# First adaptive modulation of a diffusion trunk: six chunks of 512 columns, or twelve pieces of 128, 256 and 512

## Chip, cores and metric

One core of a Trainium2 chip. The time is the device time of one execution in microseconds (us), median over runs of the same program. Inputs lie in HBM; the layout of the weights is prepared on the host ahead of the run and is not timed.

## What is computed

A trunk of four layers works on 256 context tokens and 256 latent tokens of 1024 features: a gated mixer (SGU), an RWKV7 layer, a latent attention (MLA), and a second SGU. Every layer starts in the same way, here cut to what matters for the first:

```python
def ada_modulation(cond, w, b):
    m = jax.nn.silu(cond) @ w + b            # w: 1024 x 3072
    shift, scale, gate = jnp.split(m, 3, axis=-1)
    return shift[..., None, :], scale[..., None, :], gate[..., None, :]
...
h  = rms_norm(x) * (1 + scale) + shift        # latent, from c
hc = rms_norm(ctx) * (1 + c_scale) + c_shift  # context, from c_ctx
...
u, v, z = jnp.split(h @ w_in, 3, axis=-1)     # w_in: 1024 x 6144
```

All arithmetic is float32. For the first layer the modulation needs the whole 12 MB weight matrix `ada_w[0]`, and nothing of the mixer can run before some block of `h` (128 of the 1024 features, for all 512 tokens) is there; that block needs its own 128 columns of shift and of scale.

## The kernel before, in words

Features lie on the 128 partitions, in 8 blocks `k`; the 512 tokens (256 context, 256 latent) lie along the free dimension. The kernel is written in a tile framework: the program is traced in Python order, and a list scheduler places the instructions of each engine by that order as priority and by its own estimate of when operands are ready. An engine then runs its list strictly in order, so an instruction that waits holds up what stands behind it. Tiles of one tag share a fixed number of buffers.

**Start (L1358 to L1381).** The queue of SP issues all loads: the condition, eight blocks of `xT` (256 KB each), small constants, then modulation weights and mixer weights in the order of the calls. `sq_add` sums the squares of the blocks; `norm_rstd` (L281) sums them over partitions with a matmul by ones (`ssq`) and takes the reciprocal root (`rstd`).

**Modulation (`ada_load` L201, `ada_first` L210).** `ada_w[0]` is cut into six chunks of 512 columns: chunks 0 and 1 are the shift, 2 and 3 the scale, 4 and 5 the gate. A chunk (2 MB) comes in four transfers of 512 KB, each with two of the eight `k` blocks of all 512 columns. In `ada_first` each `k` block is a matmul with the condition as stationary operand (128 x 32), in column tiles of 32, four `k` at a time into four groups of 32 partitions (`adap`, L218). ScalarE copies the result to SBUF (`m4`, L221); four matmuls with `sel2` add the four groups and transpose 128 columns each into one shared PSUM tile (`adaT`, L225); VectorE adds the bias (L228), and 1.0 for the scale (L230). The profile counts each float32 matmul as two instructions: 16 for a chunk, 8 for its transposes.

**Normalized blocks (`norm_mod` L288).** For each `k`: VectorE multiplies `xT` by `rstd` (L292); ScalarE scales and shifts the context half (L297), VectorE the latent half (L295); `split` makes the two parts of a split-float pair `hp`: a rounded part on ScalarE (L304), the rest on VectorE (L305).

**Weights (`wload` L170, `wparts` L173).** Each 1 MB of mixer weights is loaded into `raw` (3 buffers in this phase), then split into `hi` (ScalarE, L183) and `lo` (VectorE, L184), each with 2 buffers.

**First mixer, projection `v` (`sgu` L349).** Four column blocks `c` of 512, each in two halves of four `k`. For each `k` and each of four token blocks there are three matmuls (L375 to L377, tile `pv`): 48 a half, 96 a column block, 384 in all. The calls order the modulation so: `first` (L1367) runs chunks 0 and 2 and then issues the loads of chunks 1 and 3; blocks 0 to 3 are made; the first half runs; `early` runs chunks 1 and 3 and blocks 4 to 7 are made (L366 to L368); the second half runs. `later` (L1371) does the gate's chunks 4 and 5 much later. `ada_rest` (L232) computes the other layers' modulation on VectorE beside the first mixer.

Of the kernel before, what the change touches and what calls it, by code (L numbers as in the profile page):

```python
# [8 lines left out]
F32 = mybir.dt.float32  # L9
# [6 lines left out]
D = 1024  # L16
KD = 8
T = 512
RMS_EPS = 1e-6


def fm_tiles(w, kb, ob):
# [14 lines left out]
def layout(inp):  # L37
    a = {k: np.asarray(v) for k, v in inp.items()}
    o = {}
    f = np.float32  # L40
    o["xT"] = np.concatenate([a["ctx"][0], a["x"][0]], 0).T.reshape(KD, 128, T).transpose(1, 0, 2)
    o["cond"] = np.stack([cols(a["c_ctx"]), cols(a["c"][0])], -1)
    o["ada_w0"] = a["ada_w"][0].reshape(KD, 128, 6, 512).transpose(2, 1, 0, 3).reshape(6, 128, KD * 512)
    o["ada_wT"] = a["ada_w"][1:4].transpose(0, 2, 1).reshape(3, 12, 2, 128, D).transpose(0, 1, 3, 2, 4).reshape(3, 12, 128, 2 * D)
    o["condr"] = np.stack([a["c_ctx"], a["c"][0]])[None]
    o["ada_b"] = np.stack([cols(a["ada_b"][i]) for i in range(4)], 1)
    for j in range(2):
        w = a["sgu_w_in"][j]
        o[f"sgu_u{j}"] = fm_tiles(w[:, 0:2048], 8, 2)
        o[f"sgu_v{j}"] = tm_tiles(w[:, 2048:4096], 4)  # L50
        o[f"sgu_z{j}"] = fm_tiles(w[:, 4096:6144], 8, 2)
        o[f"sgu_o{j}"] = np.concatenate([fm_tiles(a["sgu_w_out"][j][i * D:(i + 1) * D], 8, 2) for i in range(2)])
        o[f"sgu_gain{j}"] = cols(a["sgu_gain"][j])
        o[f"sgu_ws{j}"] = a["sgu_w_s"][j].transpose(2, 0, 1)
        o[f"sgu_bs{j}"] = np.broadcast_to(a["sgu_b_s"][j][None], (128, 8, 128))
    for c, nm in ((0, "r"), (1, "k"), (3, "z")):
        o["rw_" + nm] = fm_tiles(a["rwkv_w_in"][0, c], 8, 2)
    o["rw_v"] = tm_tiles(a["rwkv_w_in"][0, 2], 4)
    o["rw_o"] = fm_tiles(a["rwkv_w_out"][0], 8, 2)
    for nm in "wa":  # L60
        o[f"rw_{nm}1"] = fm_tiles(a[f"rwkv_{nm}_lora1"][0].transpose(1, 0, 2).reshape(D, 128), 8, 1)
        o[f"rw_{nm}2"] = np.tile(a[f"rwkv_{nm}_lora2"][0].transpose(1, 0, 2), (2, 1, 1))
    o["rw_vec"] = np.stack([cols(a["rwkv_mu"][0, c]) for c in range(6)]
                           + [cols(a["rwkv_w0"][0, n]) for n in range(2)] + [cols(a["rwkv_a0"][0, n]) for n in range(2)]
                           + [cols(a["rwkv_" + nm][0]) for nm in ("k_k", "k_a", "r_k", "ln_gain", "ln_bias")], 1)
    t64 = np.arange(64)
    strict, incl = (t64[:, None] < t64[None, :]).astype(f), (t64[:, None] <= t64[None, :]).astype(f)
    o["masks"] = np.tile(np.concatenate([strict, incl], 1), (2, 1))
    o["bd"] = np.kron(np.eye(2, dtype=f), np.ones((64, 64), f))
    w = a["mla_w_in"][0]  # L70
    o["ml_cq"] = fm_tiles(w[:, 0:768], 8, 1)
    o["ml_ckv"] = fm_tiles(w[:, 768:1024], 8, 1)
    wr = w[:, 1024:1088]
    o["ml_kr"] = fm_tiles(np.concatenate([wr, wr], 1), 8, 1)
    o["ml_z"] = fm_tiles(w[:, 1088:3136], 8, 1)
    uq = a["mla_w_uq"][0].reshape(768, 16, 192)
    o["ml_qn"] = fm_tiles(np.ascontiguousarray(uq[:, :, 0:128]).reshape(768, 2048), 6, 1)
    o["ml_qr"] = fm_tiles(np.ascontiguousarray(uq[:, :, 128:192]).reshape(768, 1024), 6, 1)
    ukv = a["mla_w_ukv"][0].reshape(256, 16, 256)
    o["ml_kv"] = np.concatenate([fm_tiles(np.ascontiguousarray(ukv[:, :, 0:128]).reshape(256, 2048), 2, 2),  # L80
                                 tm_tiles(np.ascontiguousarray(ukv[:, :, 128:256]).reshape(256, 2048), 2, 256)], 2)
    o["ml_o"] = np.concatenate([fm_tiles(a["mla_w_out"][0][i * D:(i + 1) * D], 8, 1) for i in range(2)])
    gq, gk = a["mla_qk_gain_q"][0], a["mla_qk_gain_k"][0]
    o["ml_vec"] = np.concatenate([cols(a["mla_q_norm"][0]), cols(a["mla_kv_norm"][0])]
                                 + [np.stack([g[0:128], np.tile(g[128:192], 2)], 1) for g in (gq, gk)], 1)
    ti = np.arange(256)
    inv = (10000.0 ** (-np.arange(16, dtype=f) / f(16))).astype(f)
    ang = np.concatenate([(ti // 64).astype(f)[:, None] * inv, (ti % 64).astype(f)[:, None] * inv], 1)
    o["rope"] = np.stack([np.tile(fn(ang).astype(f).T, (4, 1)) for fn in (np.cos, np.sin)], 1)
    sw = np.zeros((64, 64), f)  # L90
    sw[np.arange(32) + 32, np.arange(32)] = -1.0
    sw[np.arange(32), np.arange(32) + 32] = 1.0
    o["swap"] = np.kron(np.eye(2, dtype=f), sw)
    o["ident"] = np.eye(128, dtype=f)
    o["sel2"] = (np.arange(128)[:, None] % 32 == np.arange(2)[None, :]).astype(f)
    return {k: np.ascontiguousarray(v) for k, v in o.items()}


def body(tc, I, out):
    nc = tc.nc  # L100
# [4 lines left out]
    def ps(name, tag=None):  # L105
        tag = tag or env["ps"][0][0]
        return env["pp"].tile([128, 512], F32, tag=tag, name=name, bufs=dict(env["ps"])[tag])
# [93 lines left out]
    def ada_load(chunks):  # L201

        raws = {}
        for n in chunks:
            for q in range(4):
                raws[n, q] = env["a"].tile([128, 2, T], F32, tag="p", name="adaw", bufs=env["npair"])
                nc.sync.dma_start(out=raws[n, q].rearrange("p k c -> p (k c)"), in_=I["ada_w0"][n, :, q * 1024:q * 1024 + 1024])
        return raws

    def ada_first(chunks, raws):  # L210

        pt = ps("adaT")
        for n in chunks:
            pm = ps("adap")
            for h in range(2):
                for kk in range(4):
                    k = h * 4 + kk
                    PE.matmul(pm[32 * kk:32 * kk + 32, :], scp[:, k, :], raws[n, k // 2][:, k % 2, :],  # L218
                              start=(h == 0), stop=(h == 1), tile_position=(0, 32 * kk))
            m4 = at("m4")  # L220
            S.copy(m4, pm)  # L221
            yield
            for q in range(4):
                f = n * 4 + q
                PE.matmul(pt[:, 2 * f:2 * f + 2], m4[:, q * 128:(q + 1) * 128], sel2, start=True, stop=True)  # L225
            f = slice(n * 4, n * 4 + 4)
            for c in range(2):
                V.tensor_tensor(mods[0][:, f, c], pt[:, 0:48].rearrange("p (f c) -> p f c", c=2)[:, f, c], ada_b[:, 0, f], ALU.add)  # L228
            if n in (2, 3):
                V.tensor_scalar(mods[0][:, f, :], mods[0][:, f, :], 1.0, None, ALU.add)  # L230

    def ada_rest():  # L232
# [113 lines left out]
            yield  # L346


    def sgu(j, m, t0, done=None, first=None, early=None, later=(), head=None):  # L349
        later = iter(later)  # L350
        n = T - t0
        tbs = list(range(t0 // 128, 4))
        r = norm_rstd(t0)
        head = head or wload(I[f"sgu_v{j}"][0])
        if first:
            first()
        hs = [pair("hp") for _ in range(KD)]
        norm_mod(m, t0, hs, r, range(4 if early else 8))
        ss = const.tile([128, 4, 4], F32, tag="ss", name="ss")
        v = {}  # L360
        for c in range(4):
# [1 line left out]
                next(later, None)  # L363
            pv = {tb: ps("pv") for tb in tbs}
            for half in range(2):
                if early and (c, half) == (0, 1):  # L366
                    early()
                    norm_mod(m, t0, hs, r, range(4, 8))  # L368
                whi, wlo = wload(I[f"sgu_v{j}"][c * 2 + half]) if c + half else head
                for kk in range(4):  # L370
                    k = half * 4 + kk
                    for tb in tbs:
                        sl = slice(tb * 128, tb * 128 + 128)
                        ws_ = slice(kk * 512, kk * 512 + 512)
# [983 lines left out]
    with phase("0", 4, 20, 3):  # L1358
        scp = silu_cond()
        for k in range(KD):  # L1360
            sq_add(k, 0)
        act_set("natural_log_exp_and_others")
        raws = ada_load((0,))
        head0 = wload(I["sgu_v0"][0])
        raws.update(ada_load((2,)))

        def first():  # L1367
            interleave(ada_first((0, 2), raws))
            raws.update(ada_load((1, 3)))

        def later():  # L1371
            r4 = ada_load((4,))
            yield
            yield from ada_first((4,), r4)
            r5 = ada_load((5,))
            yield
            yield
            yield from ada_first((5,), r5)

        sgu(0, mods[0], 0, first=first, early=lambda: interleave(ada_first((1, 3), raws)), later=later(), head=head0)  # L1380
        for _ in ada_rest():  # L1381
            pass
    rwkv(mods[1])
# [21 lines left out]
```

## Time and profile before

| what | value |
|---|---|
| median of 3 runs | 1618.8 us (1617.66 to 1621.54) |
| profiled execution, its own time | 1616.74 us |
| its span (first to last instruction) | 1615.0 us |
| TensorE busy (PE) | 1516.5 us, 94% |
| VectorE busy (DVE) | 1151.3 us, 71% |
| ScalarE busy (ACT) | 788.0 us, 49% |
| mean granted clock of TensorE | 0.97 of full |

PE is TensorE, PEld its weight loads, DVE VectorE, ACT ScalarE, SP the engine that issues the transfers. L218 is line 218 of the kernel. Each row of a timeline gives the start and the duration in us, engine, line, operation, output<-input with the shape, the count, and in brackets how long the engine stood idle before and what ended that. Matmuls are pipelined, so their durations overlap; the distance of their starts is what they cost in a dense stream. PEclk is the granted clock as a share of 2.4 GHz; 0.50 is 1.2 GHz.

### The profile page before, as it was taken

How to read it: one execution, taken by the hardware profiler on the slowest of the kernel's cores; microseconds unless marked ns; L12 is line 12 of the kernel's file. 1: busy time of each engine (PE TensorE's matmuls, PEld its weight loads, DVE VectorE, ACT ScalarE, POOL GpSimd, SP SyncE). 2: the span in 40 equal slices, each digit the busy share in tenths (PEclk: the TensorE clock that was granted, in tenths of full speed). 3: DMA queues.
4: the chain of work that ended last, by engine and by line, in shares of the span. 5: the costliest groups of instructions: out<-in, count | busy, mean ns of one | idle time of the engine just before them, and what ended most of it. 6: DMA issues, size and time to landing. Idle time of an engine off the chain costs nothing.

```text
span 1615.0 us, 28890 instructions
## 1 busy us (share of the span) xinstructions
PE 1516.5 (94%) x11666; PEld 1173.8 (73%) x11666; DVE 1151.3 (71%) x2101; ACT 788.0 (49%) x1404; POOL 124.8 (8%) x156
## 2 busy tenths in 40 slices
PE   5999999999599998899899899899999999979998
PEld 2787888888467644777676677678777777768887
DVE  3789998845788367586796854778766666665876
ACT  4544231222455353444445333569866766456543
POOL 0000000000500142212303000000000000000000
PEclk8999999999799999799999999999999999989999
DMA  9676658631044553432433133134321232265452
GB/s 366 242 288 232 234 192 305 233 105 52 36 145 167 174 159 77 145 90 80 126 103 87 59 113 103 62 129 137 121 76 47 78 92 92 66 234 196 169 183 79
DMA packets 95174, 229.05 MB, mean 142 GB/s; under 512 B 26048, under 2 KB 52160, under 8 KB 80576
## 3 DMA queue, kind: packets, MB, share of 16 engines
q1 hardware_dynamic: 92736, 223.00, 41.1%
q10 hardware_dynamic: 2304, 4.20, 0.7%
q8 instruction: 92, 1.51, 0.4%
q14 instruction: 42, 0.34, 0.1%
HBM read 208.81 MB, written 17.83 MB: 140 GB/s over the span
## 4 chain that ended last, share of the span: by engine, by line
PE 46%; DVE 6%; ACT 6%; issue 1%; POOL 1%; DMA 0%; ACTq 0%; DVEq 0%; POOLq 0%
PE fm L310 4%; PE op L310 4%; PE pg L904 3%; PE op L975 2%; PE fm L311 2%; PE op L311 2%; PE pz L310 2%; PE pu L310 2%; PE po L1286 2%; PE sc L1304 2%; PE pe L790 2%; PE sc L1305 1%; PE pv L376 1%; PE pz L311 1%; PE pv L377 1%
## 5 line engine op out<-in xcount | busy, mean ns | idle before, releaser
L184 DVE TENSOR_TENSOR lo<-raw,hi 128x2048 fp32r<-128x2048 f32 (+3 forms) x147 | 247.2, 1683 | 105.0 <-ACT hi L183 104.4
L183 ACT CAST hi<-raw 128x2048 fp32r<-128x2048 f32 (+3 forms) x161 | 212.3, 1324 | 218.8 <-PE op L314 40.5
L251 DVE SCALAR_TENSOR_TENSOR junk<-adaw,scb 128x1024 f32<-128x1024 f32 x112 | 136.9, 1222 | 13.6 <-DMA adaw<-in_ada_wT 11.7
L310 PE MATMUL op<-s,hi 128*128 128x512 f32 x256 | 91.6, 400 | 0.0
L375 PE MATMUL pv<-hi,hp 128*128 128x512 f32 x192 | 76.6, 401 | 9.1 <-ACT hi L183 6.0
L376 PE MATMUL pv<-lo,hp 128*128 128x512 f32 x192 | 76.4, 398 | 1.7 <-DVE lo L184 1.7
L310 PE MATMUL fm<-hx,hi 128*128 128x512 f32 x200 | 73.8, 409 | 4.1 <-ACT hx L304 3.8
L377 PE MATMUL pv<-hi,hp 128*128 128x512 f32 x192 | 76.2, 397 | 0.0
L904 PE MATMUL pg<-xz,wz 128*128 128x256 f32 x256 | 71.1, 412 | 0.0
L311 PE MATMUL op<-s,lo 128*128 128x256 f32 x256 | 71.1, 280 | 0.0
L313 PE MATMUL pj<-xs,hi 128*128 128x512 f32 x128 | 53.9, 423 | 12.3 <-ACT xs L304 10.2
L794 DVE TENSOR_TENSOR E<-pe,masks 128x512 f32<-128x512 f32 x64 | 41.6, 683 | 26.6 <-PE pe L790 23.9
L695 POOL TENSOR_TENSOR BK<-f 64x256 f32<-64x256 f32 x64 | 56.5, 882 | 44.3 <-DVE f L688 31.2
L311 PE MATMUL fm<-hx,lo 128*128 128x256 f32 x200 | 56.5, 287 | 2.0 <-DVE lo L184 2.0
L1004 PE MATMUL pv<-wv,xv 128*128 128x512 f32 x128 | 57.3, 596 | 0.0
L310 PEld LDWEIGHTS op<-s,hi 128*128 128x128 f32 x256 | 48.1, 188 | 12.6 <-issue 1.3
L314 PE MATMUL pj<-xs,hi 128*128 128x512 f32 x128 | 52.7, 412 | 4.0 <-DVE xs L305 4.0
L310 PE MATMUL fm<-cq,hi 128*128 128x512 f32 x144 | 55.7, 423 | 0.0
L904 PEld LDWEIGHTS pg<-xz,wz 128*128 128x128 f32 x256 | 47.1, 197 | 11.5 <-issue 3.6
L975 PE MATMUL op<-Y,wo 128*128 128x256 f32 x192 | 53.8, 415 | 1.3 <-DVE xT L979 1.3
L315 PE MATMUL pj<-xs,lo 128*128 128x512 f32 x128 | 52.5, 412 | 2.2 <-DVE lo L184 2.1
L313 PE MATMUL pu<-hp,hi 128*128 128x512 f32 x128 | 50.7, 396 | 0.0
(392 smaller groups left out, 4027.3 us busy)
## 6 DMA issues: line engine op xcount, KB each, us to landing
adaw<-in_ada_wT SPq DMA_DIRECT2D x36, 1024.0 KB, 6.2
raw<-in_sgu_v SPq DMA_DIRECT2D x16, 1024.0 KB, 5.9
raw<-in_sgu_u SPq DMA_DIRECT2D x16, 1024.0 KB, 5.3
raw<-in_sgu_z SPq DMA_DIRECT2D x16, 1024.0 KB, 5.0
raw<-in_sgu_o SPq DMA_DIRECT2D x16, 1024.0 KB, 4.8
adaw<-in_ada_w SPq DMA_DIRECT2D x24, 512.0 KB, 10.2
xz<-xz SPq DMA_DIRECT2D x32, 256.0 KB, 3.9
raw<-in_ml_z SPq DMA_DIRECT2D x16, 512.0 KB, 3.7
```

The source lines that it names most:

```text
L183: S.copy(hi[:, sl], raw[:, sl])
L184: (nc.gpsimd if parts > 1 and i else V).tensor_tensor(lo[:, sl], raw[:, sl], hi[:, sl], ALU.subtract)
L251: V.scalar_tensor_tensor(out=junk, in0=raw[:, f, :], scalar=1.0, in1=scb[:, c, :], op0=ALU.mult, op1=ALU.mult, accum_out=m[:, t * 2 + f, c ...
L310: PE.matmul(p, whi, x, start=start, stop=False)
L311: PE.matmul(p[:, 0:256], wlo, x[:, 0], start=False, stop=stop)
L313: PE.matmul(p, whi, x[:, 0], start=start, stop=False)
L375: PE.matmul(pv[tb], hs[k][:, 0, sl], whi[:, ws_], start=k == 0, stop=False)
L376: PE.matmul(pv[tb], hs[k][:, 0, sl], wlo[:, ws_], start=False, stop=False)
L377: PE.matmul(pv[tb], hs[k][:, 1, sl], whi[:, ws_], start=False, stop=k == 7)
L904: PE.matmul(p, ws[k // 4][:, k % 4, pr * 128:pr * 128 + 128], xs[k // 2][:, k % 2, :], start=k == 0, stop=k == 7)
L975: PE.matmul(p[:, ob], w[:, k, ob, :], y[:, k], start=k == 0, stop=k == 1)
L1004: PE.matmul(p, xv[:, k, tb * 128:tb * 128 + 128], ws[k // 4][:, k % 4, :], start=k == 0, stop=k == 7)
```

## The change

The columns of `ada_w[0]` are cut anew, into a list of twelve pieces: shift and scale alternate, first in pieces of 128 columns (pieces 0 to 3: blocks 0 and 1), then of 256 (pieces 4 to 9: blocks 2 to 7), then the gate in two of 512 (10 and 11). A piece is loaded in transfers of 512 KB as before: one for 128 columns (all eight `k`), two for 256, four for 512. All loads of shift and scale are now issued ahead of the mixer, with the head weights of the first half behind piece 1 and those of the second half behind piece 7. Inside the first column block, `early(k)` runs pieces 0 to 3 ahead of `k` = 0 and makes blocks 0 and 1; pieces 4 and 5 ahead of `k` = 1 and makes blocks 2 and 3; pieces 6 and 7 ahead of `k` = 3 and makes blocks 4 and 5; pieces 8 and 9 ahead of `k` = 5 and makes blocks 6 and 7. Only the columns of a piece are multiplied, copied and transposed. The second SGU layer passes no `early` and is as before.

```diff
@@ -18,6 +18,8 @@
 T = 512
 RMS_EPS = 1e-6
 
+PIECES = [(c + s, n) for c, n in ((0, 128), (128, 128), (256, 256), (512, 256), (768, 256)) for s in (0, D)] + [(2 * D, 512), (2 * D + 512, 512)]
+
 
 def fm_tiles(w, kb, ob):
     n = w.shape[1] // (ob * 128)
@@ -40,7 +42,8 @@
     f = np.float32
     o["xT"] = np.concatenate([a["ctx"][0], a["x"][0]], 0).T.reshape(KD, 128, T).transpose(1, 0, 2)
     o["cond"] = np.stack([cols(a["c_ctx"]), cols(a["c"][0])], -1)
-    o["ada_w0"] = a["ada_w"][0].reshape(KD, 128, 6, 512).transpose(2, 1, 0, 3).reshape(6, 128, KD * 512)
+    w0 = a["ada_w"][0].reshape(KD, 128, 3 * D)
+    o["ada_w0"] = np.concatenate([w0[:, :, c:c + n].transpose(1, 0, 2).reshape(128, KD * n) for c, n in PIECES], 1)
     o["ada_wT"] = a["ada_w"][1:4].transpose(0, 2, 1).reshape(3, 12, 2, 128, D).transpose(0, 1, 3, 2, 4).reshape(3, 12, 128, 2 * D)
     o["condr"] = np.stack([a["c_ctx"], a["c"][0]])[None]
     o["ada_b"] = np.stack([cols(a["ada_b"][i]) for i in range(4)], 1)
@@ -202,31 +205,33 @@
 
         raws = {}
         for n in chunks:
-            for q in range(4):
-                raws[n, q] = env["a"].tile([128, 2, T], F32, tag="p", name="adaw", bufs=env["npair"])
-                nc.sync.dma_start(out=raws[n, q].rearrange("p k c -> p (k c)"), in_=I["ada_w0"][n, :, q * 1024:q * 1024 + 1024])
+            at0, w = sum(w for _, w in PIECES[:n]) * KD, PIECES[n][1]
+            raws[n] = []
+            for q in range(w // 128):
+                t = env["a"].tile([128, 1024 // w, w], F32, tag="p", name="adaw", bufs=env["npair"])
+                nc.sync.dma_start(out=t.rearrange("p k c -> p (k c)"), in_=I["ada_w0"][:, at0 + q * 1024:at0 + q * 1024 + 1024])
+                raws[n] += [t[:, k, :] for k in range(1024 // w)]
         return raws
 
     def ada_first(chunks, raws):
 
         pt = ps("adaT")
         for n in chunks:
+            c0, w = PIECES[n]
             pm = ps("adap")
             for h in range(2):
                 for kk in range(4):
                     k = h * 4 + kk
-                    PE.matmul(pm[32 * kk:32 * kk + 32, :], scp[:, k, :], raws[n, k // 2][:, k % 2, :],
-                              start=(h == 0), stop=(h == 1), tile_position=(0, 32 * kk))
+                    PE.matmul(pm[32 * kk:32 * kk + 32, 0:w], scp[:, k, :], raws[n][k], start=(h == 0), stop=(h == 1), tile_position=(0, 32 * kk))
             m4 = at("m4")
-            S.copy(m4, pm)
+            S.copy(m4[:, 0:w], pm[:, 0:w])
             yield
-            for q in range(4):
-                f = n * 4 + q
-                PE.matmul(pt[:, 2 * f:2 * f + 2], m4[:, q * 128:(q + 1) * 128], sel2, start=True, stop=True)
-            f = slice(n * 4, n * 4 + 4)
+            f = slice(c0 // 128, (c0 + w) // 128)
+            for q in range(w // 128):
+                PE.matmul(pt[:, 2 * (f.start + q):2 * (f.start + q) + 2], m4[:, q * 128:(q + 1) * 128], sel2, start=True, stop=True)
             for c in range(2):
                 V.tensor_tensor(mods[0][:, f, c], pt[:, 0:48].rearrange("p (f c) -> p f c", c=2)[:, f, c], ada_b[:, 0, f], ALU.add)
-            if n in (2, 3):
+            if D <= c0 < 2 * D:
                 V.tensor_scalar(mods[0][:, f, :], mods[0][:, f, :], 1.0, None, ALU.add)
 
     def ada_rest():
@@ -346,16 +351,15 @@
             yield
 
 
-    def sgu(j, m, t0, done=None, first=None, early=None, later=(), head=None):
+    def sgu(j, m, t0, done=None, early=None, later=(), head=None):
         later = iter(later)
         n = T - t0
         tbs = list(range(t0 // 128, 4))
         r = norm_rstd(t0)
         head = head or wload(I[f"sgu_v{j}"][0])
-        if first:
-            first()
         hs = [pair("hp") for _ in range(KD)]
-        norm_mod(m, t0, hs, r, range(4 if early else 8))
+        if not early:
+            norm_mod(m, t0, hs, r, range(8))
         ss = const.tile([128, 4, 4], F32, tag="ss", name="ss")
         v = {}
         for c in range(4):
@@ -363,12 +367,15 @@
                 next(later, None)
             pv = {tb: ps("pv") for tb in tbs}
             for half in range(2):
-                if early and (c, half) == (0, 1):
-                    early()
-                    norm_mod(m, t0, hs, r, range(4, 8))
-                whi, wlo = wload(I[f"sgu_v{j}"][c * 2 + half]) if c + half else head
+                if early and c == 0:
+                    whi, wlo = next(head)
+                else:
+                    whi, wlo = wload(I[f"sgu_v{j}"][c * 2 + half]) if c + half else head
                 for kk in range(4):
                     k = half * 4 + kk
+                    if early and c == 0:
+                        for kn in early(k):
+                            norm_mod(m, t0, hs, r, [kn])
                     for tb in tbs:
                         sl = slice(tb * 128, tb * 128 + 128)
                         ws_ = slice(kk * 512, kk * 512 + 512)
@@ -1360,24 +1367,29 @@
         for k in range(KD):
             sq_add(k, 0)
         act_set("natural_log_exp_and_others")
-        raws = ada_load((0,))
-        head0 = wload(I["sgu_v0"][0])
-        raws.update(ada_load((2,)))
-
-        def first():
-            interleave(ada_first((0, 2), raws))
-            raws.update(ada_load((1, 3)))
+        raws = ada_load((0, 1))
+        head0 = [wload(I["sgu_v0"][0])]
+        raws.update(ada_load((2, 3, 4, 5, 6, 7)))
+        head0.append(wload(I["sgu_v0"][1]))
+        raws.update(ada_load((8, 9)))
+
+        def early(k):
+
+            n, ks = {0: ((0, 1, 2, 3), (0, 1)), 1: ((4, 5), (2, 3)), 3: ((6, 7), (4, 5)), 5: ((8, 9), (6, 7))}.get(k, ((), ()))
+            if n:
+                interleave(ada_first(n, raws))
+            return ks
 
         def later():
-            r4 = ada_load((4,))
+            r4 = ada_load((10,))
             yield
-            yield from ada_first((4,), r4)
-            r5 = ada_load((5,))
+            yield from ada_first((10,), r4)
+            r5 = ada_load((11,))
             yield
             yield
-            yield from ada_first((5,), r5)
-
-        sgu(0, mods[0], 0, first=first, early=lambda: interleave(ada_first((1, 3), raws)), later=later(), head=head0)
+            yield from ada_first((11,), r5)
+
+        sgu(0, mods[0], 0, early=early, later=later(), head=iter(head0))
         for _ in ada_rest():
             pass
     rwkv(mods[1])
```

## Rows read from the trace of the kernel before

**Rows 1.** The page, part 1: busy us, share, instructions.
```profile
PE 1516.5 (94%) x11666; PEld 1173.8 (73%) x11666; DVE 1151.3 (71%) x2101; ACT 788.0 (49%) x1404; POOL 124.8 (8%) x156
```
**Rows 2.** Busy time by stretch: from:to, length, engines, clock, transfers' share, GB/s.
```profile
0.00:30.43 30.43, 13.52 (x50) 3.85 (x50) 10.91 (x22) 14.34 (x21) 0.75 (x9) 0.91 0.94 353
...
60.86:126.45 65.59, 65.59 (x290) 54.05 (x288) 59.61 (x79) 27.90 (x48) 0.00 (x0) 1.00 0.73 270
...
180.00:200.00 20.00, 20.00 (x90) 16.55 (x89) 19.85 (x28) 4.88 (x7) 0.00 (x0) 1.00 0.64 227
...
380.00:400.00 20.00, 20.00 (x90) 16.57 (x89) 8.90 (x14) 4.34 (x5) 0.00 (x0) 1.00 0.28 106
```
**Rows 3.** Timeline up to the first mixer matmuls.
```profile
16.80 0.19 PEld L218 LDWEIGHTS adap<-adaw,scp 128*32 128x32 f32 x4 [1.02 <-DMA adaw<-in_ada_w]
...
19.28 1.90 ACT L183 CAST hi<-raw 128x2048 fp32r<-128x2048 f32 x1 [0.31 <-DMA raw<-in_sgu_v]
...
21.21 2.29 DVE L184 TENSOR_TENSOR lo<-raw,hi 128x2048 fp32r<-128x2048 f32 x1 [0.87 <-ACT hi L183]
...
24.42 0.19 PEld L218 LDWEIGHTS adap<-adaw,scp 128*32 128x32 f32 x4 [1.09 <-DMA adaw<-in_ada_w]
25.62 0.59 ACT L221 COPY m<-adap 128x512 f32<-128x512 f32 x1 [4.43 <-PE adap L218]
...
26.25 1.05 PE L225 MATMUL adaT<-sel,m 128*128 128x2 f32 x8 [0.69 <-ACT m L221]
...
28.29 1.58 ACT L297 ACTIVATE h<-h,mod 128x256 f32<-128x256 f32 x3 [2.09 <-DVE mod L230]
...
29.78 1.64 ACT L304 CAST hp<-h 128x512 fp32r<-128x512 f32 x3
...
30.43 0.79 PE L375 MATMUL pv<-hi,hp 128*128 128x512 f32 x1 [3.12 <-ACT hp L304]
...
34.87 0.42 PE L376 MATMUL pv<-lo,hp 128*128 128x512 f32 x1
```
**Rows 4.** Timeline of the second pair of chunks.
```profile
43.32 0.39 PE L377 MATMUL pv<-hi,hp 128*128 128x512 f32 x1
...
43.64 1.92 PE L218 MATMUL adap<-adaw,scp 128*32 128x512 f32 x16
...
44.09 0.13 PEld L218 LDWEIGHTS adap<-adaw,scp 128*32 128x32 f32 x4 [0.30 <-issue]
44.52 0.13 PEld L218 LDWEIGHTS adap<-adaw,scp 128*32 128x32 f32 x4 [0.30 <-issue]
...
45.68 2.29 DVE L184 TENSOR_TENSOR lo<-raw,hi 128x2048 fp32r<-128x2048 f32 x1 [4.33 <-ACT hi L183]
...
46.29 1.05 PE L225 MATMUL adaT<-sel,m 128*128 128x2 f32 x8 [0.73 <-ACT m L221]
47.28 1.92 PE L218 MATMUL adap<-adaw,scp 128*32 128x512 f32 x16
...
49.13 0.50 PE L375 MATMUL pv<-hi,hp 128*128 128x512 f32 x1
...
49.47 0.40 PE L376 MATMUL pv<-lo,hp 128*128 128x512 f32 x1
...
50.17 0.95 PE L225 MATMUL adaT<-sel,m 128*128 128x2 f32 x8
...
50.98 0.47 PE L376 MATMUL pv<-lo,hp 128*128 128x512 f32 x1
```
**Rows 5.** Busy time of the tile `pv` alone, one stretch: PE, PEld, ACT, clock, transfers.
```profile
30.43:60.86 30.43, 24.36 (x96) 19.25 (x97) 0.00 (x0) 0.93 0.81 314
```
**Rows 6.** Transfers issued in the first 80 us: queue, count, KB each, us to landing.
```profile
adaw<-in_ada_w SPq DMA_DIRECT2D x16, 512.0 KB, 10.2
```
**Rows 7.** Busy time by stretch of 1 us, columns as in rows 2.
```profile
28.00:29.00 1.00, 0.00 (x0) 0.00 (x0) 0.96 (x5) 0.71 (x2) 0.00 (x0) 0.53 0.99 401
...
45.00:46.00 1.00, 0.56 (x8) 0.00 (x0) 0.32 (x1) 0.99 (x2) 0.00 (x0) 1.00 0.99 360
```

## The prediction

> **What bounds the kernel now.** I read the page first: TensorE (PE) is busy 94% of the span [rows 1], so the question is where PE stands still, not what it does. Then the table of busy time by stretch [rows 2]. In the first 30.43 us PE is busy 13.5 us, and little of that is the mixer. From 60.86 to 126.45 us it has no idle time, and the same holds at 380 to 400 us, with VectorE (DVE) at 8.90 of 20 us there and 19.85 of 20 us at 180 to 200. In none of these stretches does PE wait for DVE. So what PE gains before 60.86 us should travel through the first mixer unchanged.
>
> The timeline of the start [rows 3] shows why the first mixer matmul (`pv`) comes at 30.43 us. The transfers come in order: the fourth half-megabyte of modulation weights lets PE go at 16.80, the head weights (1 MB) their cast at 19.28, the eighth half-megabyte (chunk 2, the scale) the last PE step at 24.42. From there it is one chain: matmuls, copy to SBUF at 25.62, transposes at 26.25 to 27.30, modulation, three blocks' scaling on ScalarE (ACT) from 28.29, the first cast at 29.78, PE at 30.43. The last weights to the first mixer matmul: 6.01 us.
>
> From 30.43 the stream is dense but for the second pair of modulation chunks [rows 4]: mixer matmuls end at 43.55 (43.32 and one spacing of 0.23), return at 49.13, and stop once more from 50.17 to 50.98. That is 5.58 and 0.81 us, with 0.1 for changes of form 6.5 us. The 96 mixer matmuls of one column block fill the rest until 60.86 [rows 5]: 96 x 0.227 = 21.8; ten of them ran at half clock, until 34.87 [rows 3], 4.44 us where ten at full clock take 2.27, so 2.2 lost. 30.43 + 21.8 + 2.2 + 6.5 = 60.9 closes the account.
>
> **The change part by part.** Transfers: 16 issues of 512 KB before [rows 6]; after, four pieces of one issue and six of two, again 16, with the same 1 MB of head weights between. SP's queue carries the same count in another order, and the second half of the head now goes ahead of the last two pieces. I cost this at nothing; what hides it is a PE that from the first block on works slower than the data come: the last piece is the twentieth half-megabyte (counting both weight halves), where the transfers, 1.28 us apart (24.42 back to 19.28 for four), have it by 37.3 us. If that cover went, PE would wait there; I see it needed at 46 us or later.
>
> First block: it now needs pieces 0 to 3. The last of these is the sixth half-megabyte, landed by 19.28 [rows 3]. Of the 6.01 us chain, two transposes in place of eight save 0.8; scaling two blocks and not three before the first cast 0.5; the narrow matmuls 0.4; the narrower copy 0.2 of its 0.59. 4.1 us are left, and I add 0.3 for piece 2's steps ahead of piece 3's on PE: 23.7 us. Bounds: 25.3 (the whole 6.01 chain) and 21.0, where head weights landed at 16.80 have been split (1.90 on ACT, 2.29 on DVE [rows 3]). I take 23.7, nearer the chain, because all four pieces stand ahead of block 0 in the program. **Gain 6.7 us.**
>
> Modulation inside the stream: before, two chunks of 512 columns; now six pieces of 256, since only 512 of the 2048 columns (before 1024) are done ahead of the first block. Weight loads of consecutive rounds in a 512-column chunk stand 0.43 us apart (44.09, 44.52 [rows 4]), four rounds and 0.2 over make its 1.92. At half the columns: 4 x 0.21 + 0.2 = 1.05, an estimate bounded by 0.86 (no overhead) and 1.92 (width buys nothing). Four transposes of eight: 0.41. Changing between full and column-tiled matmuls costs 0.1 each way: 43.32 to 43.64 and 49.13 to 49.47 where mixer matmuls stand 0.23 apart [rows 4]. So 1.05 + 0.41 + 0.2 = 1.66, six times 10.0 us against 6.5. **Loss 3.5 us.** The waits for the copies (0.73 before 46.29) I cost at nothing, since mixer matmuls of a block already made can fill them, as four did at 49.13.
> The Trainium skill, TensorEngine Tiling (Array Packing), section Key Properties, speaks against cutting into more pieces: changing the tiling mode drains the engine. The trace agrees, and its 0.1 us is the price; with no such drain the loss would be 1.2 us smaller after and 0.4 before, so 0.8 better in all.
>
> Half clock at the start: all twelve matmuls of block 0 instead of ten, 0.4 us more. **Loss 0.4.**
>
> Hand-offs: three times a pair of pieces must become two blocks before PE runs out: after its last transpose, 3.1 us in the old chain (27.30 to 30.43 [rows 3]), 2.6 with two blocks for three. Cover is the block behind the pair: twelve matmuls, 2.7 us, of which some three fill a copy wait; 2.0 us are left. Wait 0.5 each (0.6 by that, somewhat less since the first cast releases PE); bounds 0 and 3.8 (nothing covered: 3.1 and the copy's 0.73). Queued behind these waits are all later mixer matmuls, as PE runs in order. **Loss 1.5.** The rest is small: some 15 more short DVE operations of about 0.15 us lie beside PE work, or inside the chain above; the gate's two pieces keep place and width.
>
> Sum: 6.7 - 3.5 - 0.4 - 1.5 = **1.3 us gained.** The profiled execution took 1616.7 us, 1615.0 of it span, and would come to 1615.4; it stands 2.1 us under the median of the three runs, 1618.8, so for a median I say **1617.5 us**. A change of 0.3% (4.9 us) is about what a measurement can tell from none; I expect no difference that can be told.
>
> **The rivals.**
> (a) Blocks 0 and 1 are truly made as soon as pieces 0 and 1 are known, ahead of pieces 2 and 3, and only the head's split holds PE: first matmul at 21.2. For it: ACT and DVE stand mostly idle until then, and in the old trace DVE took work early where operands were there. Gain 9.2, modulation at 1.47 a piece (8.8, loss 2.3), half clock 0.4, hand-offs 0.3 each: 5.6 gained, **1613.2 us**. Against: four serial copies and the head's 1.90 us cast share ACT. Chance 0.25.
> (b) The other side: the hand-offs are not covered. If the pair's matmuls stand on PE behind the block that should cover them, or a weight split sits before the modulation on DVE, as the 2.29 us at 45.68 did [rows 4], then PE stands idle about 3.8 us three times: 6.7 - 3.9 - 11.4 = -8.6, **1627.4 us**. The sign turns where a hand-off costs over 0.9 us, the difference can be told from 2.6 us each. Against: the pieces land (24.42, then about 29.5 and 37) well before PE comes to them. Chance 0.15.
> (c) Clock: PE stood idle after 27.30 and the granted clock was 0.53 at 28 to 29 us, half level through the first matmuls; in the 0.7 us pause at 45 to 46 it stayed 1.00 [rows 7]. If each hand-off let it fall, three times 2.2 us: 1.3 - 6.5 = -5.2, **1624.0 us**. The Trainium skill, TensorE: Matmul & The Clock Gate, section What's actually happening, has the throttled level as the default that activity releases, which would make every pause a risk; the pause at 45 us shows that short ones are not. Chance 0.05.
> (d) The change doesn't do what it says: pieces 4 and 5 slip ahead of block 0 on PE, which then waits for the tenth half-megabyte (24.42) and their steps (1.05, 0.7, 0.41): 26.6 us. Gain 3.8, four pieces left in the stream 6.6 against 6.5, 0.4 and two hand-offs 1.0: 2.3 gained, **1616.5 us**. Chance 0.10.
>
> **How the numbers follow.** Forecast 0.45, (a) 0.25, (b) 0.15, (c) 0.05, (d) 0.10. Forecast and (d) lie within 0.3%: 0.55. Faster is (a): 0.25. Slower is (b) and (c): 0.20. The range runs from 1611.0, under (a) with the lower bounds of the pieces, to 1624.5, just past (c); it leaves out (b) and little else.
>
> **What would show it.** First `pv` at 23 to 24.5 us (21 is (a), 26 or later (d)). The 96th `pv` at about 59.6 in place of 60.86. A 256-column piece at about 1.05 us in the table of its tile; 1.9 would make the change slower. Waits of `pv` for the cast of `hp` under 1 us each; three of 3 us and more is (b). Granted clock 1.00 from some 5 us after the first `pv`, or (c). From there to 400 us the old trace, shifted. I am wrong in kind if the shift at 60 us and that of the end differ by more than 3 us: then something later waits that I took for covered.

## The result, and the profile after

The changed kernel takes **1627.62 us** (median of 6 runs, 1624.29 to 1628.6) beside 1618.76 us for the kernel before (6 runs, 1613.83 to 1621.54): a ratio of **1.0052, 95% interval 1.0034 to 1.007**. (Ratios here and below are the ones on record with their intervals; they can differ from the quotient of the two medians, by up to 0.0015.) It is slower by about 8 us, where I had forecast no difference that can be told and a range that ended at 1624.5 us. The profiled execution took 1627.28 us, 1625.5 of it span, against 1616.7 and 1615.0 before.

First the page, part 1, of the changed kernel, which answers to [rows 1]. PE is busy for 3.1 us less than before (1513.4 against 1516.5 us), so its idle time has grown by more than the 10.5 us of the span.

```profile
PE 1513.4 (93%) x11762; PEld 1175.0 (72%) x11762; DVE 1152.4 (71%) x2116; ACT 788.5 (49%) x1410; POOL 125.9 (8%) x156
```

Then busy time by stretch, columns as in [rows 2], with the first stretch cut at the new first `pv` and the second begun just behind the start of its 96th (70.55 us). What the clock column says of the first stretch is taken up in the last section.

```profile
0.00:34.96 34.96, 8.40 (x74) 4.86 (x74) 11.00 (x25) 15.47 (x23) 0.75 (x9) 1.00 0.93 344
...
70.65:126.45 55.80, 55.70 (x246) 45.81 (x245) 52.15 (x72) 24.80 (x43) 0.00 (x0) 1.00 0.77 283
180.00:200.00 20.00, 20.00 (x98) 16.87 (x97) 19.31 (x29) 5.22 (x7) 0.00 (x0) 1.00 0.58 208
380.00:400.00 20.00, 20.00 (x89) 16.30 (x88) 10.02 (x14) 8.05 (x8) 0.00 (x0) 1.00 0.29 106
```

PE is idle for 26.6 of the first 34.96 us (34.96 less 8.40); before it was 16.9 of 30.43. Behind 70.65 us it is dense again. So the loss lies ahead of the stream, and the timeline of that stretch, which answers to [rows 3], says where:

```profile
23.22 0.56 PE L231 MATMUL adaT<-sel,m 128*128 128x2 f32 x2 [0.78 <-DVE mod L233]
...
25.06 0.60 ACT L302 ACTIVATE h<-h,mod 128x256 f32<-128x256 f32 x1 [0.69 <-DVE h L297]
...
32.49 1.90 ACT L186 CAST hi<-raw 128x2048 fp32r<-128x2048 f32 x1 [6.83 <-DMA raw<-in_sgu_v]
34.30 1.14 ACT L309 CAST hp<-h 128x512 fp32r<-128x512 f32 x2
34.42 2.29 DVE L187 TENSOR_TENSOR lo<-raw,hi 128x2048 fp32r<-128x2048 f32 x1 [8.95 <-ACT hi L186]
34.96 0.80 PE L382 MATMUL pv<-hi,hp 128*128 128x512 f32 x1 [11.19 <-ACT hp L309]
...
36.63 1.29 DVE L310 TENSOR_TENSOR hp<-h,hp 128x512 fp32r<-128x512 f32 x2
37.37 0.79 PE L384 MATMUL pv<-hi,hp 128*128 128x512 f32 x1 [1.19 <-DVE hp L310]
```

ACT has scaled blocks 0 and 1 by 25.66 us (DVE its half by 25.48), and nothing that ACT needs for their casts is missing. Yet the casts (L309) start at 34.30. Ahead of them ACT has the cast of the second half of the head weights (L186), which waits 6.83 us for its transfer, and ACT takes its instructions in order. DVE has the same order: the `lo` of that weight half (34.42 to 36.71) stands ahead of the rests of `hp` (36.63), for which PE waits another 1.19 us. PE's own wait is 11.19 us.

The list of waits, from 13 to 72 us, puts the three side by side (total, times, longest):

```profile
PE pv L382 <- ACT hp L309: 11.2, 1, 11.2
DVE lo L187 <- ACT hi L186: 10.7, 3, 8.9
...
ACT hi L186 <- DMA raw<-in_sgu_v: 6.8, 1, 6.8
```

One wait of `pv` for a cast of `hp`, not three; with the 1.2 us for the rest of block 0 it is all that the stream has, and from block 1 on it has none. Its two other views, the busy time of the tile `pv` ([rows 5] before) and the pieces inside the stream, with their matmuls and transposes, which answer to [rows 4]:

```profile
34.96:70.60 35.64, 27.25 (x96) 18.77 (x97) 0.00 (x0) 1.00 0.63 236
```
```profile
41.38 0.63 PE L384 MATMUL pv<-hi,hp 128*128 128x512 f32 x1
...
41.94 1.07 PE L225 MATMUL adap<-adaw,scp 128*32 128x256 f32 x16
42.94 0.50 PE L382 MATMUL pv<-hi,hp 128*128 128x512 f32 x1
...
43.73 0.50 PE L231 MATMUL adaT<-sel,m 128*128 128x2 f32 x4
...
44.17 1.07 PE L225 MATMUL adap<-adaw,scp 128*32 128x256 f32 x16
45.17 0.50 PE L382 MATMUL pv<-hi,hp 128*128 128x512 f32 x1
```

From the first to the 96th matmul it is some 35.6 us in place of 30.4, and they start 4.53 us later: the 96th starts 9.7 us later (70.55 against 60.85). That shift passes on. The last matmuls of the first SGU's output projection, by the tile `op` between 300 and 440 us (durations in ns, then first and last start), first of the kernel before, then of the changed one:

```profile
L315 PE MATMUL op<-s,lo x64: 387/389/397, 364.9 to 408.0; 128*128 128x512 f32 x64
```
```profile
L320 PE MATMUL op<-s,lo x64: 387/389/397, 375.0 to 418.1; 128*128 128x512 f32 x64
```

10.1 us there, 10.5 in the span. The transfers kept their count, as in [rows 6]:

```profile
adaw<-in_ada_w SPq DMA_DIRECT2D x16, 512.0 KB, 10.2
```

### The profile page after: what moved, and what is told of

Its sections match the earlier page's. It is cut to its first block, busy times and chain, and to the rows that moved or that the text cites. A ratio compares the mean times of both kernels' runs of the same rounds, so it can differ in the third digit from the quotient of the medians.

```text
span 1625.5 us, 29117 instructions
## 1 busy us (share of the span) xinstructions
PE 1513.4 (93%) x11762; PEld 1175.0 (72%) x11762; DVE 1152.4 (71%) x2116; ACT 788.5 (49%) x1410; POOL 125.9 (8%) x156
## 4 chain that ended last, share of the span: by engine, by line
PE 46%; DVE 7%; ACT 5%; issue 1%; POOL 1%; DMA 1%; ACTq 0%; DVEq 0%; POOLq 0%
PE fm L315 5%; PE op L315 4%; PE pg L911 2%; PE fm L316 2%; PE op L982 2%; PE op L316 2%; PE pz L315 2%; PE pu L315 2%; PE po L1293 2%; PE sc L1311 2%; PE pe L797 2%; PE sc L1312 1%; PE pv L383 1%; PE pv L384 1%; PE pz L316 1%
## 5 line engine op out<-in xcount | busy, mean ns | idle before, releaser
L186 ACT CAST hi<-raw 128x2048 fp32r<-128x2048 f32 (+3 forms) x161 | 212.3, 1324 | 212.5 <-PE op L319 40.5
L382 PE MATMUL pv<-hi,hp 128*128 128x512 f32 x192 | 77.0, 405 | 17.2 <-ACT hp L309 11.2
L801 DVE TENSOR_TENSOR E<-pe,masks 128x512 f32<-128x512 f32 x64 | 41.5, 682 | 26.6 <-PE pe L797 24.1
L382 PEld LDWEIGHTS pv<-hi,hp 128*128 128x128 f32 x192 | 37.0, 193 | 27.7 <-ACT hp L309 11.7
L911 PEld LDWEIGHTS pg<-xz,wz 128*128 128x128 f32 x256 | 46.6, 196 | 11.3 <-issue 3.8
```

The source lines that it names most:

```text
L186: S.copy(hi[:, sl], raw[:, sl])
L382: PE.matmul(pv[tb], hs[k][:, 0, sl], whi[:, ws_], start=k == 0, stop=False)
L911: PE.matmul(p, ws[k // 4][:, k % 4, pr * 128:pr * 128 + 128], xs[k // 2][:, k % 2, :], start=k == 0, stop=k == 7)
```

## The experiments

The theory after this reading (the **cast theory**): the change puts the load of the second weight half, and with it its cast, ahead of the first use; in ACT's list the cast then stands ahead of the casts of blocks 0 and 1, and they wait for a transfer that they do not need. The rival (the **piece theory**): more and smaller pieces hold PE by themselves, through their hand-offs between PE, ACT and DVE. Times of before beside the first four kernels: 1617.1 us (29 runs); beside the last three: 1617.68 us (29 runs).

The order of an engine's list is made when the program is built, by priority and by an estimate of when operands are ready. So the edits do not rely on the place of the source line alone; they name the instruction behind which another is to be issued (`tc.issue_after`).

**swap_cast.** The second half is loaded where the change loads it, and cast behind the casts of blocks 0 and 1.

```diff
-        head0.append(wload(I["sgu_v0"][1]))
+        head1 = wload_late(I["sgu_v0"][1])     # same load; returns the function that splits it
...
+            with tc.issue_after(state["after"].ins):   # cast of hp, block 1
+                S.copy(hi, raw)
```

> The changed kernel, but on ScalarE the cast of the second 1 MB of mixer weights stands behind the first two casts of hp and no longer ahead of them; its transfer stays where it is. Theory A (this one cast, waiting for its transfer at 32.5 us, holds the first mixer matmul back to 35.0 us): first pv at about 25.1 us (block 0 is scaled at 24.4). The cast then waits in the same way ahead of the copies of pieces 4 and 5, which come only at about 34.5 us, so PE stands still again for some 2 us there: the 96th pv about 7.5 us earlier than in the changed kernel, 1620 us (1618 to 1622). Theory B (the pieces themselves cost the time: six in the mixer's stream, more changes of form; the start is only moved): first pv earlier, but the end within 2 us of the changed kernel, 1626 to 1629.

Measured: 1619.48 us (12 runs, 1615.63 to 1625.01), ratio 1.0006 [0.999, 1.0022]. Timeline:

```profile
26.09 0.79 PE L398 MATMUL pv<-hi,hp 128*128 128x512 f32 x1 [2.45 <-ACT hp L323]
...
33.44 1.90 ACT L182 CAST hi<-raw 128x2048 fp32r<-128x2048 f32 x1 [6.88 <-DMA raw<-in_sgu_v]
35.37 2.29 DVE L183 TENSOR_TENSOR lo<-raw,hi 128x2048 fp32r<-128x2048 f32 x1 [8.01 <-ACT hi L182]
35.66 0.61 PE L245 MATMUL adaT<-sel,m 128*128 128x2 f32 x4 [2.48 <-ACT m L241]
```

The first `pv` comes 8.87 us sooner than in the changed kernel (34.96 less 26.09), and by the two ratios some 7 us of the 8 are back (1.0052 against 1.0006). They hung on the place of one cast in ACT's list (its `lo` on DVE moved with it). The cast still waits 6.88 us, and now the copy of piece 4 (`m`) stands behind it: PE has a wait of 2.48 us one block further on.

**late_cast.** The same with the cast behind those of blocks 2 and 3 (the condition `kn == 1` made `kn == 3`).

> As the run before, but the cast stands behind the casts of blocks 2 and 3, so that nothing of the first three blocks waits for that transfer. Theory A: first pv at about 25.1 us, no wait of the copies of pieces 4 and 5, the 96th pv at 25.1 + 21.8 + 2.6 (half clock) + 10 (pieces) = 59.5 us against 60.9 in the kernel before: 1617.5 us (1615.5 to 1619.5), that is no change that can be told from the kernel before. Theory B: 1626 to 1629.

Measured: 1622.29 us (12 runs, 1617.87 to 1628.94), ratio 1.0033 [1.0013, 1.0054], a miss: no better than swap_cast (the intervals overlap), and slower than before. Timeline:

```profile
26.34 0.80 PE L398 MATMUL pv<-hi,hp 128*128 128x512 f32 x1 [2.45 <-ACT hp L323]
...
43.42 0.17 DVE L414 TENSOR_SCALAR gh<-sgu_gain 128x16 f32<-128x16 f32 x1 [5.64 <-DMA sgu_gain<-in_sgu_gain]
43.50 1.28 DVE L324 TENSOR_TENSOR hp<-h,hp 128x512 fp32r<-128x512 f32 x2
...
44.24 1.22 PE L400 MATMUL pv<-hi,hp 128*128 128x512 f32 x2 [4.07 <-DVE hp L324]
```

The cast no longer waits for its transfer, but the same thing happens on DVE: the halving of the SGU's gain (L414, 0.17 us of work, first used at 162.7 us) stands ahead of the rests of `hp` and waits 5.64 us for its transfer; PE waits 4.07 us for them. Such a wait costs more than its length: during it the granted clock fell to 0.50 (0.50 throughout 43 to 49 us), and the eight matmuls behind it (44.24 to 47.40) start 0.43 us or more apart. The cast theory was too narrow: it holds for any instruction whose operand comes late.

**before_cast_first.** The cross-check: the kernel *before*, its pieces untouched, with the second half's load and split traced ahead of blocks 0 to 3 (the transfer keeps its place in SP's queue) and the first `hp` cast held behind that cast.

```diff
+            head0.append(wload(I["sgu_v0"][1]))
+            state["first"] = state.pop("w")            # its cast
...
+            with tc.issue_after(state.pop("first").ins):
+                S.copy(x[:, 0], src)                    # first hp cast
```

> The kernel before, with six chunks and its order of transfers, and only this added: on ScalarE the cast of the second half's weights stands ahead of the first cast of hp. Theory A: the cast waits for its transfer, landed at 37.1 us in the kernel before, takes 1.9, and the first pv comes at about 39.7 us in place of 30.4; the rest shifts by 9.2 us: 1628 us (1626.5 to 1630). Theory B: a late start alone costs little, 1619 to 1622.

Measured: 1632.16 us (6 runs, 1627.76 to 1634.32), ratio 1.0078 [1.0051, 1.0104]. Timeline:

```profile
37.41 1.90 ACT L183 CAST hi<-raw 128x2048 fp32r<-128x2048 f32 x1 [6.97 <-DMA raw<-in_sgu_v]
...
39.88 0.79 PE L379 MATMUL pv<-hi,hp 128*128 128x512 f32 x1 [12.01 <-ACT hp L306]
...
54.12 1.90 ACT L183 CAST hi<-raw 128x2048 fp32r<-128x2048 f32 x1 [8.74 <-PE pv L381]
...
59.77 0.37 PE L225 MATMUL adaT<-sel,m 128*128 128x2 f32 x1 [3.83 <-ACT m L221]
```

With not one piece more, the old kernel gets the wait (12.01 us) and the loss: the piece theory does not need to be called on. It lost more than the start alone: of 17.4 us of span (1632.4 less 1615.0) the start is 9.45 (39.88 less 30.43). Another 3.1 is PE's wait of 3.83 (0.73 before) for a copy that stands behind the cast of the third weight half, which waits 8.74 us for PE. In that wait the granted clock fell (0.50 at 60 to 66 us), and the transposes and the second chunk's matmuls behind it lasted 1.87 and 3.64 us where they had lasted 1.05 and 1.92: 2.5 more. The other 2.3 us I did not take apart.

**early_load.** The changed kernel, ACT's list as it is, with the second half's transfer ahead of pieces 4 to 7.

```diff
-        raws.update(ada_load((2, 3, 4, 5, 6, 7)))
+        raws.update(ada_load((2, 3)))
         head0.append(wload(I["sgu_v0"][1]))
-        raws.update(ada_load((8, 9)))
+        raws.update(ada_load((4, 5, 6, 7, 8, 9)))
```

> The changed kernel with the same order on ScalarE, but the second half's weights are transferred ahead of pieces 4 to 7 and not behind them. Theory A: they land about 8 half-megabytes after the first piece, near 23 us, the cast runs at 25.7 to 27.6 behind the scaling of block 1, the first pv comes at 28.2 us, 6.8 us earlier than in the changed kernel, and all that follows with it: 1621 us (1619 to 1623). If hp waits for a buffer or for something other than this cast, the first pv stays near 35 us and the time near 1627.

Measured: 1619.03 us (12 runs, 1614.42 to 1624.66), ratio 1.0006 [0.9985, 1.0027]. Timeline:

```profile
25.39 1.88 ACT L186 CAST hi<-raw 128x2048 fp32r<-128x2048 f32 x1
27.17 1.14 ACT L309 CAST hp<-h 128x512 fp32r<-128x512 f32 x2
...
27.84 0.79 PE L382 MATMUL pv<-hi,hp 128*128 128x512 f32 x1 [4.25 <-ACT hp L309]
30.25 0.79 PE L384 MATMUL pv<-hi,hp 128*128 128x512 f32 x1 [1.19 <-DVE hp L310]
```

The other way to the same end: leave the order, let the operand come sooner. PE did not need the transfer that early; the cast did, at the place where it stands in ACT's list. The start is 1.75 us later than swap_cast's, since ACT still takes the weight cast first (1.88 us, from 25.39), now without a wait.

**held_order.** late_cast, with everything else of that kind held behind the casts and rests of blocks 6 and 7: the gain and bias of the SGUs, the constants of the RWKV layer, the tanh of the second modulation's input, the casts of the third and fourth weight halves.

```diff
+        with tc.issue_after(state["made"].ins):         # rest of hp, block 7
             V.tensor_scalar(gh, gain, 0.5, None, ALU.mult)
             V.tensor_scalar(bh, bs, 0.5, None, ALU.mult)
...
+            with tc.issue_after(state["done"].ins):     # cast of hp, block 7
                 S.activation(t, scb, AF.Tanh, scale=0.5)
```

> As late_cast, and everything on ScalarE and VectorE that waits for a later transfer or for later work of TensorE (the gain and bias of both SGUs, the constants of the RWKV layer, the tanh of the second modulation's input, the cast of the next two weight halves) is held behind the casts and rests of blocks 6 and 7. The cast theory, widened to any instruction whose operand comes late and that stands ahead in an engine's list: first pv at 26.3 us as in late_cast, no wait of TensorE for hp over 1 us behind it, matmuls at full rate from about 31.5 us on, the 96th pv ends at 26.3 + 21.8 (96 matmuls) + 2.6 (half rate at the start) + 9.9 (six pieces) = 60.6 us against before's 60.85, so the time of before within 0.15%: 1616.5 to 1620 us, ratio 1.000 (0.9985 to 1.0015). The rival that the pieces themselves and their hand-offs hold TensorE: the waits of late_cast for hp come back at the same blocks with another releaser, the 96th pv stays at 64 us or later, ratio 1.002 to 1.0035.

Measured: 1613.69 us (12 runs, 1611.96 to 1619.02), ratio 0.9978 [0.9968, 0.9988]: faster than before, where I had expected the same. PE's timeline from the first `pv` on shows every wait that is left, and the 96th `pv`:

```profile
25.83 0.80 PE L405 MATMUL pv<-hi,hp 128*128 128x512 f32 x1 [2.45 <-ACT hp L325]
...
46.42 0.50 PE L405 MATMUL pv<-hi,hp 128*128 128x512 f32 x1 [0.45 <-ACT hp L325]
...
59.58 0.39 PE L407 MATMUL pv<-hi,hp 128*128 128x512 f32 x1
```

The stream is dense but for 0.45 us, and the hand-offs cost next to nothing. The 96th starts 1.3 us ahead of before (59.58 against 60.85). It ends at 59.8 (59.58 and one spacing), 0.8 ahead of what I expected, as this execution's `ssq` began 0.5 us sooner than late_cast's and full rate came sooner: from 28.95 on, behind seven matmuls of block 0, the starts are 0.23 us apart. The rest of its lead arose later (last section). Several instructions were held at once here; which of them had cost PE time besides the gain's halving, the run does not separate.

**block0_first.** held_order, with block 0 made right behind pieces 0 and 1, ahead of block 1.

```diff
-            n, ks = {0: ((0, 1, 2, 3), (0, 1)), 1: ((4, 5), (2, 3)), 3: ((6, 7), (4, 5)), 5: ((8, 9), (6, 7))}.get(k, ((), ()))
-            if n:
+            for n, ks in {0: (((0, 1), (0,)), ((2, 3), (1,))), 1: (((4, 5), (2, 3)),), 3: (((6, 7), (4, 5)),), 5: (((8, 9), (6, 7)),)}.get(k, ()):
...
+            with (tc.issue_after(state["rest"].ins) if "scale" in state and k else ExitStack()):
+                V.tensor_tensor(h[:, t0:T], xT[:, k, t0:T], r[:, t0:T], ALU.mult)
...
+                    with (tc.issue_after(state["scale"].ins) if "scale" in state else ExitStack()):
+                        S.activation(h[:, a:b], h[:, a:b], AF.Identity, scale=m[:, 8 + k, c:c + 1], bias=m[:, k, c:c + 1])
...
+                            if kn < 2:
+                                state["scale"] = state["cast"] if kn else state["hi0"]
```

> As held_order, and block 0 is made right behind pieces 0 and 1, ahead of block 1: its scale on ScalarE behind the cast of the first weight half, its cast ahead of block 1's scale, its rest ahead of block 1's multiplication by rstd. The cast theory: TensorE goes from the transposes of piece 3 (23.3 us) into the stream within 1 us, first pv at 24.0 us (23.4 to 25.0), the 96th pv at 24.0 + 21.8 + 2.6 + 9.9 = 58.3 us (57.8 to 59.5), 1.3 to 3 us ahead of before, and that lead passes to the end: ratio 0.9985 (0.998 to 0.9992). The rival that the lead is given back (transfers of the weights that come next, or of pieces 6 to 9, end last instead): first pv as said, but waits of TensorE for a DMA or for casts of weights by 55 us, ratio 1.000 or above. The rival that hand-offs hold the stream: a wait of 1 to 3 us for hp at block 1, 96th pv at 60.5 us or later.

Measured: 1613.42 us (12 runs, 1607.65 to 1616.82), ratio **0.9966 [0.9952, 0.9981]**, the lowest here. PE's timeline:

```profile
22.42 0.58 PE L246 MATMUL adaT<-sel,m 128*128 128x2 f32 x2 [0.44 <-ACT m L242]
22.94 0.80 PE L410 MATMUL pv<-hi,hp 128*128 128x512 f32 x1
...
44.88 0.50 PE L410 MATMUL pv<-hi,hp 128*128 128x512 f32 x1 [0.45 <-ACT hp L327]
...
58.10 0.39 PE L412 MATMUL pv<-hi,hp 128*128 128x512 f32 x1
```

PE goes from the transposes of piece 3 into the stream with no wait at all: 22.94, 7.49 us sooner than before. That is the start that the change was made for, and it needs the order on ACT and DVE. Of the 2.9 us that it starts ahead of held_order, 1.5 are left at the 96th `pv` (58.10 against 59.58), because all its first twelve matmuls went at the low rate, and only seven of held_order's: full rate came at nearly the same time in both, behind 28.12 here and from 28.95 there. The intervals of the two ratios overlap: that block0_first beats held_order is not shown, that both beat before is.

**narrow_pieces.** held_order with pieces 4 to 9 cut from six of 256 columns to twelve of 128.

```diff
-PIECES = [(c + s, n) for c, n in ((0, 128), (128, 128), (256, 256), (512, 256), (768, 256)) ...
+PIECES = [(c + s, n) for c, n in [(i * 128, 128) for i in range(8)] ...
```

> As held_order, and pieces 4 to 9 (six of 256 columns) are cut to twelve of 128 columns: the same columns and bytes, twice the hand-offs and changes of TensorE's form. First pv unchanged at 26.3 us. The cast theory, by which a piece costs its own matmuls, transposes and changes of form and no wait: between 12 x (0.54 + 0.21 + 0.2) = 11.4 and 12 x (1.08 + 0.21 + 0.2) = 17.9 us of pieces in place of 9.9, as the eight matmuls of a piece of 128 columns take half or all of the 1.07 us of one of 256; 96th pv 1.5 to 8 us behind held_order, taken 2.5, ratio to before about 1.0015. The rival by which each hand-off costs a wait of 0.5 to 3.8 us: waits of TensorE for hp or m of that length at blocks 2 to 7 in the list of waits, six more of them, so 3 to 23 us on top.

Measured: 1616.97 us (12 runs, 1612.47 to 1626.19), ratio 1.0008 [0.9989, 1.0026]. PE's timeline, a pair of pieces and the 96th `pv`:

```profile
30.63 0.65 PE L240 MATMUL adap<-adaw,scp 128*32 128x128 f32 x16
31.78 0.28 PE L246 MATMUL adaT<-sel,m 128*128 128x2 f32 x2
...
34.13 0.38 PE L246 MATMUL adaT<-sel,m 128*128 128x2 f32 x2 [0.15 <-ACT m L242]
...
61.45 0.39 PE L407 MATMUL pv<-hi,hp 128*128 128x512 f32 x1
```

From first to 96th `pv` it takes 35.82 us against held_order's 33.75: 2.1 us for six more pieces, 0.3 each, beside 2.5 expected. A piece's matmuls went from 1.07 to 0.65 us, and the longest wait for a copy in the stream is 0.15 us. Six more hand-offs cost no wait; for the stream the piece theory is out.

## Why the prediction was wrong, point by point

**The start, 23.7 us: wrong, and the whole of the miss.** It came at 34.96, 11.3 us late; the other terms together came out about as forecast. The step that failed is the first one: "the second half of the head now goes ahead of the last two pieces. I cost this at nothing", with as cover that PE would need the last piece "at 46 us or later". I asked when PE needs the transfers, and counted the move on SP's queue alone. But the load moves its cast and its `lo` with it, and these went into ACT's and DVE's lists ahead of the casts and rests of block 0. What counts is not when PE needs them but when ACT comes to them: the data landed at 32.5 us, and ACT came to the cast at 25.7. The landing could have been told from the prediction's own spacing: in the new order that half ends as the sixteenth half-megabyte, six behind the tenth at 24.42, so at 32.1. [Rows 4] had the warning: the `lo` at 45.68 waited 4.33 us on `ACT hi`, a weight cast in the middle of the modulation's steps. I used that row for rival (b) and not for the item that was being moved.

With the cast away from there, the first `pv` comes at 25.6 to 26.3 us (four runs): some 9 of the 11.3 us were the cast's. It is still 1.9 to 2.6 later than 23.7. I took the last weights, at 19.28, as what the chain hangs on; it hangs on PE. The four pieces run one behind another from the end of `ssq` on: in held_order their transposes start at 16.49, 18.47, 20.46 and 22.82, each piece's matmuls behind the copy and transposes of the one before. They ran at the lower rate there, 1.08 us a piece (last section). And `ssq` itself began later (12.79 us in held_order, 13.31 in late_cast, 11.91 before). block0_first shows that 22.94 is to be had.

**Pieces in the stream, 6 x 1.66 = 10.0: right.** The matmuls of a piece lasted 1.07 us (1.05 predicted), transposes 0.44 from start to the next step (0.41). Read from PE's starts, as what the six pieces add to the distances between mixer matmuls, they cost 9.9 us, and the two chunks before 6.6 (6.5 in the prediction).

**Half clock, 0.4: right.** All twelve matmuls of block 0 went at the lower rate, as said, 0.43 us apart but for the first after each wait; before it was ten.

**Hand-offs, 3 x 0.5 = 1.5: too dear.** No wait at a hand-off in the changed kernel, one of 0.45 us in held_order.

**The rivals.** (b) gave 1627.4 us, and 1627.6 came, but by another mechanism: I had a weight split before the modulation on DVE, three times, at 3.8 us each hand-off. It was one wait, of 11.2 us, at the start, on ACT first. The right kind of obstacle with the wrong place and price; its number is an accident. (a) came nearest in block0_first: the start at 22.94, not 21.2. (c) and (d) did not occur: from 43.27 on the mixer matmuls stand 0.23 us apart, and PE does pieces 4 and 5 behind block 0.

**The passing on: right.** 9.7 us at the end of the stream, 10.1 at 400 us, 10.5 at the end. A loss at the start is paid in full. A gain is kept as well: block0_first is 2.8 us ahead at the 96th `pv` and 2.9 in the span. held_order's 1.3 had become 3.2 by the end, in part by a step of the second layer, in part by what was not found (last section).

With the terms as read from PE's starts the sum closes: the start lost 4.5 (30.43 to 34.96), the wait at 37.37 1.4 (37.37 in place of 35.99), the pieces 3.3 and the half clock 0.4, together 9.6, beside the 9.7 that the stream shows.

## What to carry to other kernels

When a load is moved, follow the instructions that unpack it into the list of the engine that runs them, and ask what stands behind them there: an in-order engine makes everything behind such an instruction as late as its transfer. An operation of 0.17 us whose result nobody used for over 100 us cost PE 4 us in this way, so constants and later weights belong behind the casts that PE waits for, by an order that is set and not hoped for. And removing one such wait shows the next: look at the waits again after each.

## What the runs showed that was not expected

**Where the trace has no clock record, the clock column says 1.00.** In the changed kernel (busy time by stretch) the column says 1.00 in a stretch whose matmuls stand 0.43 us apart; in the kernel before, at much the same spacing (ten in 4.44 us), it says 0.50:

```profile
38.00:41.00 3.00, 3.00 (x9) 2.32 (x8) 0.00 (x0) 0.00 (x0) 0.00 (x0) 1.00 1.01 421
```
```profile
32.43:34.87 2.44, 2.44 (x8) 1.85 (x7) 1.47 (x3) 1.22 (x2) 0.00 (x0) 0.50 1.05 431
```

The starts in the first are 38.39, 38.82, 39.24 and so on, where full rate is 0.227 apart. That is the rate of the lower level, 1.2 GHz. The column does not contradict it: the records of the granted clock in this trace begin only at 41.92 us, with the full level, and a stretch without a record is shown as 1.00. From 41.94 on PE works at full rate. The long idle time of PE (23.78 to 34.96 us) need not have lowered the clock: it was at the lower rate ahead of it too, as piece 0 shows, whose sixteen matmuls took 1.08 us where a piece of the same form takes 0.65 in narrow_pieces, at a recorded 1.00:

```profile
15.17 1.08 PE L225 MATMUL adap<-adaw,scp 128*32 128x128 f32 x16
```

In the start of a kernel the spacing of like matmuls is the safer reading.

**The same clock moves a step of the second layer by 1 us from one profiled execution to another.** Behind the first SGU one `ssq` matmul stands alone on PE. ACT's wait for it, in the timelines of before and of held_order:

```profile
412.97 0.69 ACT L278 ACTIVATE rstd<-ssq,eps 128x512 f32<-128x512 f32 x1 [2.96 <-PE ssq L283]
```
```profile
410.73 0.69 ACT L299 ACTIVATE rstd<-ssq,eps 128x512 f32<-128x512 f32 x1 [2.00 <-PE ssq L304]
```

The granted clock is 0.59 at 410 to 412 us in the first and 1.00 at 408.7 to 410.7 in the second, with the same work ahead of it. Of the nine kernels, each profiled once, three waited 2.0 us, two 2.1 and 2.3, and four 2.95 to 2.96; held_order is among the first and block0_first among the last. This is 1.0 of the 3.2 us by which held_order's span is shorter, beside 1.3 from the stream (its shift at the first SGU's end); where the other 0.9 arose, in the layers behind, was not found, and stays open.
